# Split parts instead of activations through DRAM, and another order at the turn of the passes, in a hybrid decoder layer

## The chip, the cores and the metric

The kernel runs on one core of one Trainium2 chip. The metric is the device time in microseconds of one execution of the whole layer. Times below come from three runs, and from one further execution that the hardware profiler recorded.

## The reference

One decoder layer over 256 tokens of width 2048 in float32: a combined projection, two groups of eight attention heads (differential attention, and block attention that with 256 tokens is causal attention over one block), an output projection, LayerNorm, a gated FFN of width 5632 with a causal convolution of three taps, and a second LayerNorm. The change touches the FFN's down projection and what stands around it:

```python
def conv_ffn(h, w_up, conv_w, conv_b, w_down):
    u = h @ w_up
    g, val = u[..., :FFN_DIM], u[..., FFN_DIM:]
    ...
    gc = conv_b + sum(conv_w[j] * gp[:, j:j + S] for j in range(CONV_W))
    return (jax.nn.silu(gc) * val) @ w_down
...
f = conv_ffn(h, w_up[l], conv_w[l], conv_b[l], w_down[l])
h = layer_norm(DEEPNORM_ALPHA * h + f, ln2_g[l], ln2_b[l])
```

## The kernel before

**Precision.** A float32 operand is split in two fp32r parts: `hi`, a rounded copy (ScalarE), and `lo`, the operand less `hi` (VectorE). A product of two operands is three matmuls: hi by hi, hi by lo, lo by hi.

**Stream.** The weights come as a list of steps, `stream`, of 1 MB each: v, q/k, o, the up projection's g and u, and the down projection's d. Each step's weights are loaded by SyncE (`load`, lines L128 and L129 for a d step) into one of four `raw` tiles, which rotate, and split by `split` (L179 on ScalarE, L181 on VectorE) into one of six hi and six lo tiles.

**Down projection.** The inner dimension of 5632 makes 44 tiles of 128, taken as 22 pairs p (`PT`). The output of 256 x 2048 is more than the eight PSUM banks hold beside the shared products, so its columns are done in two passes n of 1024. A pass has the four blocks `CB[t][c]` (two row halves t, two column blocks c) in banks 0 to 3.

- *First pass (n = 0).* Pairs 0 to 19 are multiplied between the matmuls of the up projection (`up_step`, four steps a pair, q and s in the code; `down_products`), each by seven block products in place of eight (Winograd's form; the sums of activations in `side["s"]`, their parts in `side["sh"]` and `side["sl"]`). Banks 4 to 7 (`MB`) take the products that several blocks share. Pairs 20 and 21 follow as plain steps at `first_d` and `first_d` + 1.
- *Turn.* `z_add` adds the first pass's banks into the residual `z` (L1231), and `shared_out` adds the shared products (L1237, L1241, L1244). The second pass writes the same banks.
- *Second pass (n = 1).* The 22 pairs again, in order j = 0 to 21. Steps j = 2, 5, 8, 11, 14 are by seven products (`mm_seven`, 21 matmuls, blocks of weights prepared by `blocks_raw`, `blocks_lo`, `blocks_sum`, `blocks_hi` in `slot`), the others plain (`mm_d`, 24 matmuls). The last four pairs (`PAIRED_END`) are run column block by column block, so that the second LayerNorm can start.

**Activations.** `act_out` leaves a pair's activations in a ring of three. For the second pass `act_spill` (L506) writes them to DRAM (`spilled`, 256 KB a pair), and `act_back` (L513) reads them into `back` five steps ahead, on SyncE's queue in front of the weight load. `split_act` (L564 on ScalarE, L565 on VectorE) splits the two halves of a pair again, and for a seven-product step `act_sums` and `act_sums_split` (L583 to L586, L603, L604) form and split the sums again. The raw blocks' `lo` of a seven-product step is made by ScalarE's negated copy (L624) and an accumulating transfer from POOL's queue (L625).

**Order.** Each engine runs its instructions in the order in which the program issues them; waits are put in by the framework from the tiles' uses. `begin(i)` and `middle(i)` hold the preparation of step i + 2 (and the first half of i + 3); `at(i, ...)` hangs work on a step, run by `pending` after that step's splits. At step j = 9, `load_gb` (L467) loads the second LayerNorm's gain and bias, 1 MB each, on SyncE's queue. All matmuls of the projections are recorded at line L277.

The turn's work is hung on its steps by

```python
for part in range(2):
    at(first_d + part, shared_out, 0, part)
```

Of the kernel before, what the change touches and what calls it, by code (L numbers as in the profile page):

```python
# [11 lines left out]
F32 = mybir.dt.float32  # L12
# [40 lines left out]
ENDS = {(1, 1): ("cos_d", "sin_d"), (2, 0): ("mask", "lam4"), (2, 1): ("cos_m", "sin_m")}  # L53
# [6 lines left out]
def hymba_layer(ctx: ExitStack, tc: tile.TileContext, a: dict):  # L60
# [38 lines left out]
    for j, p in enumerate((*range(PT - LATE, PT), *range(PT - LATE))):  # L99
        stream.append(("d", p, 1, j))  # L100
# [133 lines left out]
    cst = {}  # L234

    def load_table(n):
        t = keep.tile([P, S], F32, name=n)
        SP.dma_start(t, a[n])
        cst[n] = t

    def load_consts():
        for n in ("cos_d", "sin_d", "mask"):
            load_table(n)
        lam4 = keep.tile([P, 4, SUB], F32, name="lam4")
# [244 lines left out]
    def act_ring():  # L489

        if "ring" not in kept:
            t = kept["ring"] = keep.tile([P, 4096], F32, name="ring", tag="mb")
            kept["raw"], kept["gb"] = t[:, 1536:3584], t[:, 3584:]
            kept["spilled"] = dram.tile([PT - LATE, P, 2, S], F32, name="spilled")
        return kept["ring"][:, 0:1536].rearrange("p (n k t) -> p n k t", k=2, t=S)
# [4 lines left out]
    def act_of(i, k):  # L500

        _, p, n, _ = stream[i]
        return kept["back"][:, p % 7, k] if n == 1 and p < PT - LATE else act_pair(p)[:, k]

    def act_spill(p):
        SP.dma_start(kept["spilled"][p], act_pair(p))  # L506

    def act_back(i):
        if i >= NS or stream[i][2] == 0 or stream[i][1] >= PT - LATE:
            return  # L510
        if "back" not in kept:
            kept["back"] = keep.tile([P, 8, 2, S], F32, name="back", tag="big")
        SP.dma_start(kept["back"][:, stream[i][1] % 7], kept["spilled"][stream[i][1]])  # L513
# [22 lines left out]
    aparts = {}  # L536
# [5 lines left out]
    def act_tiles(i, k):  # L542

        late = i - (NS - PAIRED_END)
        if (late, k) in ENDS:
            return [keep.tile([P, S], F32R, name="eh", tag=g) for g in ENDS[late, k]]
        if k == 0 and late < 3:
            return [work.tile([P, STAND_AT + S], F32R, name=n, tag=g, bufs=3)[:, STAND_AT:]
                    for n, g in (("ah", "e0"), ("al", "e1"))]
        if late < 1:  # L550
            return work.tile([P, S], F32R, name="bh", tag="pt"), work.tile([P, S], F32R, name="bl", tag="on")
        if k == 1 and i > first_d:
            both = work.tile([P, 2, S], F32R, name="chl", tag="sh", bufs=1)
        else:
            both = work.tile([P, 2, S], F32R, name="dhl", tag="m1")
        return both[:, 0], both[:, 1]

    def split_act(i, k):

        if i >= NS or stream[i][0] != "d" or (i, k) in aparts:  # L560
            return
        src = act_of(i, k)
        hi, lo = act_tiles(i, k)
        ACT.activation(hi, src, AF.Copy)  # L564
        DVE.tensor_tensor(lo, src, hi.bitcast(F32), ALU.subtract)  # L565
        aparts[i, k] = (hi, lo)
# [3 lines left out]
    sums = {}  # L570
    gap = []

    def act_sums(i):
        kind, p, _, _ = stream[i]
        if kind == "v":
            x = [xraw[:, k * S:(k + 1) * S] for k in (2 * p + 1, 2 * p)]
            f = work.tile([P, 2, 2, P], F32, name="vf", tag="sh", bufs=1)
            f = [f[:, 0], f[:, 1]]
        else:
            x = [act_of(i, k) for k in range(2)]  # L580
            f = [keep.tile([P, 2, P], F32, name="sf", tag=g) for g in ("cos_m", "sin_m")]
# [3 lines left out]
        DVE.tensor_tensor(f[1][:, 0], f[0][:, 1], a11, ALU.add)  # L585
        DVE.tensor_tensor(f[1][:, 1], a12, f[1][:, 0], ALU.subtract)  # L586
        sums[i] = f

    def act_sums_split(i):
        f = sums[i]  # L590
        out = []
        for j in range(2):
            if stream[i][0] == "d":
                hi = keep.tile([P, 2, P], F32R, name="sh", tag=("cos_d", "mask")[j])
                lo = keep.tile([P, 2, P], F32R, name="sl", tag=("sin_d", "lam4")[j])
            else:
                o = (STAND_AT, 0)[j]
                if j == 1 and not gap:

                    gap.append(work.tile([P, 8], F32, name="gap", bufs=1))  # L600
                hi, lo = (work.tile([P, o + S], F32R, name=n, tag=g, bufs=b)[:, o:].rearrange("p (k t) -> p k t", t=P)
                          for n, g, b in ((("vh", "e0", 3), ("vl", "e1", 3)), (("wh", "pt", 2), ("wl", "on", 2)))[j])
            ACT.activation(hi, f[j], AF.Copy)  # L603
            DVE.tensor_tensor(lo, f[j], hi.bitcast(F32), ALU.subtract)  # L604
            out += [(hi[:, k], lo[:, k]) for k in range(2)]

        sums[i] = out
# [3 lines left out]
    def blocks_raw(i):  # L611
# [3 lines left out]
        if kind == "d":  # L615
            slot = keep.tile([P, 2, 7, 512], F32R, name="slot", tag="t2")
            hi, lo = slot[:, 0], slot[:, 1]
# [6 lines left out]
        ACT.activation(lo[:, 0:3], t[:, 0:3], AF.Copy, scale=-1.0)  # L624
        POOL.dma_start(lo[:, 0:3], t[:, 0:3], accum_op=ALU.add)  # L625
# [10 lines left out]

    def blocks_sum(i, j):
# [5 lines left out]
        if j == 1:  # L643
            loaded.pop(i)
# [75 lines left out]
    def down_tiles():  # L720
# [3 lines left out]
        side["sh"] = [keep.tile([P, 2, P], F32R, name="sh", tag=g) for g in ("cos_d", "mask")]  # L724
        side["sl"] = [keep.tile([P, 2, P], F32R, name="sl", tag=g) for g in ("sin_d", "lam4")]
        side["x"] = [work.tile([P, S], F32R, name="xp", tag="pt") for _ in range(2)]
        side["a"] = work.tile([P, STAND_AT + S], F32R, name="ap", tag="e0", bufs=3)[:, STAND_AT:]
# [20 lines left out]
    def down_products(p):  # L748
        t, r, a1, (xh_, xl_) = side["t"], side["r"], side["a"], side["x"]
        sh, sl = side["sh"], side["sl"]  # L750
        (s3, s1), (s2, s4) = ([(sh[j][:, k], sl[j][:, k]) for k in range(2)] for j in range(2))
        a11, a12, a22 = (a1[:, 0:P], a1[:, P:]), (xh_[:, 0:P], xl_[:, 0:P]), (xh_[:, P:], xl_[:, P:])
# [33 lines left out]
    def begin(i):  # L786
# [3 lines left out]
        split_act(j - 1, 1)  # L790
        split_act(j, 0)
# [3 lines left out]
        elif j - 1 < NS and seven(j - 1):  # L795
# [324 lines left out]
    def up_step(i):  # L1120
# [18 lines left out]
        if s == 0 and now:  # L1139
            if "r" not in side:  # L1140
                side["r"] = keep.tile([P, 2, 3, 512], F32R, name="rslot", tag="big")
# [55 lines left out]
        if i >= first_d - 2:  # L1197
            split_act(i + 1, 1)
            split_act(i + 2, 0)
# [8 lines left out]
        if s == 0 and q >= 1 and q - 1 < PT - LATE:  # L1208
            act_spill(q - 1)
# [17 lines left out]
    act_out(FT - 1, up_sum(first_d - 1))  # L1227

# [4 lines left out]
    def shared_out(n, part):  # L1233

        u = kept["gb"] if n == 0 else kept["back"][:, 7].rearrange("p k t -> p (k t)")
# [37 lines left out]
    for part in range(2):  # L1273
        at(first_d + part, shared_out, 0, part)
    for i in range(first_d, NS - PAIRED_END):
# [4 lines left out]
        if i == last[0] - 1:  # L1280
            split_act(last[1], 1)
            for j, g in ((last[2], "t2"), (last[3], "mb")):
                end = keep.tile([P, 4, 1024], F32R, name="end", tag=g)
                for k in range(2):
                    split_act(j, k)
# [5 lines left out]
        else:  # L1291
# [10 lines left out]
            if n == 0 and p == PT - 1:  # L1302
# [101 lines left out]
    for c in range(2):  # L1404
        s = slice(c * 512, (c + 1) * 512)
        ACT.activation(z[:, 1, s], ends[c], AF.Copy, scale=rstd)
        store(1, c * 512, (c + 1) * 512)
# [72 lines left out]
```

## Time and profile before

| | |
|---|---|
| median of 3 runs | 1130.36 us (1129.09 to 1130.74) |
| the profiled execution | 1128.65 us, its span 1126.9 us |
| mean granted TensorE clock | 0.995 |
| TensorE busy | 1110.4 us (99%), 5929 matmuls |
| VectorE, ScalarE, POOL busy | 865.0, 702.9, 48.5 us |
| moved by DMA | 254.14 MB, 226 GB/s over the span |

The span is the time from the first to the last instruction of the core; the execution's own time has some 1.8 us around it. A busy TensorE is not TensorE at its peak, as matmuls overlap, so the count of matmuls in a stretch says more than its busy time. In a row of waits, the engine and line that waited stand first, then what ended the wait, then the total, the number of waits and the longest. In a row of stretches stand the stretch and its length, then for TensorE's matmuls, its weight loads, VectorE, ScalarE and POOL the busy time with the number of instructions, then the granted clock, the share of time in which the 16 DMA engines were busy, and GB/s. In a row of a group the figures behind the bar are busy time and the mean of one in ns, then the idle time before them with what ended it. Queue q1 is that of the transfers that SyncE starts, q0 that of POOL's.

### The profile page before, as it was taken

How to read it: one execution, taken by the hardware profiler on the slowest of the kernel's cores; microseconds unless marked ns; L12 is line 12 of the kernel's file. 1: busy time of each engine (PE TensorE's matmuls, PEld its weight loads, DVE VectorE, ACT ScalarE, POOL GpSimd, SP SyncE). 2: the span in 40 equal slices, each digit the busy share in tenths (PEclk: the TensorE clock that was granted, in tenths of full speed). 3: DMA queues.
4: the chain of work that ended last, by engine and by line, in shares of the span. 5: the costliest groups of instructions: out<-in, count | busy, mean ns of one | idle time of the engine just before them, and what ended most of it. 6: DMA issues, size and time to landing. Idle time of an engine off the chain costs nothing.

```text
span 1126.9 us, 15881 instructions
## 1 busy us (share of the span) xinstructions
PE 1110.4 (99%) x5929; PEld 955.0 (85%) x5929; DVE 865.0 (77%) x1469; ACT 702.9 (62%) x1136; POOL 48.5 (4%) x61
## 2 busy tenths in 40 slices
PE   9999999999999999999999999999999999989987
PEld 7888888888888898888888888888888888868875
DVE  6776778877745779888888877777777777698776
ACT  6666776644533577666666666666666666657662
POOL 0000110000000000000000000000000000000003
PEclk9999999999999999999999999999999999999999
DMA  9889766444455448777766877777777777578962
GB/s 341 273 276 326 225 188 205 150 157 179 172 182 201 156 162 273 246 250 239 234 234 234 278 236 239 229 232 241 238 231 228 233 224 223 170 232 240 311 260 76
DMA packets 58860, 254.14 MB, mean 226 GB/s; under 512 B 5968, under 2 KB 7456, under 8 KB 40992
## 3 DMA queue, kind: packets, MB, share of 16 engines
q1 hardware_dynamic: 53600, 226.92, 56.0%
q0 software_dynamic: 5184, 26.22, 12.4%
q8 instruction: 46, 0.75, 0.3%
q14 instruction: 30, 0.25, 0.1%
HBM read 219.80 MB, written 7.08 MB: 201 GB/s over the span
## 4 chain that ended last, share of the span: by engine, by line
PE 94%; DVE 2%; DMA 1%; ACT 1%; issue 1%; SPq 0%; DVEq 0%
PE bank L277 93%; DMA back<-spilled 1%; PE bank L404 0%; DVE lo L181 0%; DVE z L1231 0%; ACT hi L179 0%; PE bank L975 0%; PE bank L451 0%; ACT hf L978 0%; ACT slot L624 0%; ACT slot L630 0%; ACT ah L564 0%; DVE h L990 0%; DVE slot L635 0%; ACT bh L564 0%
## 5 line engine op out<-in xcount | busy, mean ns | idle before, releaser
L277 PE MATMUL bank<-h,hi 128*128 128x512 f32 x1376 | 480.9, 390 | 0.0
L277 PE MATMUL bank<-h,lo 128*128 128x256 f32 x1376 | 387.9, 282 | 0.0
L277 PEld LDWEIGHTS bank<-h,hi 128*128 128x128 f32 x1376 | 258.2, 188 | 54.5
L277 PEld LDWEIGHTS bank<-h,lo 128*128 128x128 f32 x1376 | 260.0, 189 | 3.7
L181 DVE TENSOR_TENSOR lo<-raw,hi 128x1024 fp32r<-128x1024 f32 x147 | 177.9, 1222 | 83.9 <-ACT hi L179 83.2
L198 DVE TENSOR_TENSOR lo<-raw,hi 128x1024 fp32r<-128x1024 f32 x171 | 206.9, 1221 | 25.0 <-ACT hi L190 24.9
L179 ACT ACTIVATE hi<-raw 128x1024 fp32r<-128x1024 f32 x155 | 162.9, 1055 | 78.2 <-PE bank L277 54.0
L277 PE MATMUL bank<-x,hi 128*128 128x512 f32 x512 | 183.4, 399 | 0.0
L190 ACT ACTIVATE hi<-raw 128x1024 fp32r<-128x1024 f32 x171 | 177.3, 1051 | 0.0
L277 PE MATMUL bank<-x,lo 128*128 128x256 f32 x512 | 144.3, 282 | 0.0
L1095 ACT ACTIVATE ub<-bank 128x512 f32<-128x512 f32 x86 | 51.4, 598 | 111.1 <-PE bank L277 108.1
L277 PEld LDWEIGHTS bank<-x,hi 128*128 128x128 f32 x512 | 96.2, 188 | 21.9 <-issue 2.3
L277 PEld LDWEIGHTS bank<-x,lo 128*128 128x128 f32 x512 | 96.8, 189 | 0.2
L1104 DVE TENSOR_TENSOR ub<-ub 128x256 f32<-128x256 f32 x86 | 36.5, 424 | 57.8 <-ACT ub L1095 57.8
L730 ACT ACTIVATE tslot<-tf 128x512 fp32r<-128x512 f32 x80 | 50.4, 629 | 40.9 <-DVE tf L1184 22.2
L733 DVE TENSOR_TENSOR tslot<-tf,tslot 128x512 fp32r<-128x512 f32 x80 | 55.3, 691 | 12.3 <-ACT tslot L730 10.3
L277 PE MATMUL bank<-hi,x 128*128 128x512 f32 x208 | 56.5, 394 | 0.0
L277 PEld LDWEIGHTS bank<-hi,x 128*128 128x128 f32 x208 | 39.4, 190 | 8.7 <-ACT hi L210 0.3
L277 PE MATMUL bank<-hi,mh 128*128 128x512 f32 x128 | 41.2, 394 | 0.0
L277 PE MATMUL bank<-lo,mh 128*128 128x512 f32 x128 | 40.8, 390 | 0.0
L277 PE MATMUL bank<-hi,ml 128*128 128x512 f32 x128 | 40.8, 389 | 0.0
L531 ACT ACTIVATE gc<-gc 128x256 f32<-128x256 f32 x44 | 18.4, 418 | 35.0 <-DVE gc L528 35.0
(281 smaller groups left out, 1589.5 us busy)
## 6 DMA issues: line engine op xcount, KB each, us to landing
raw<-in_w_u SPq DMA_DIRECT2D x88, 1024.0 KB, 4.8
raw<-in_w_d SPq DMA_DIRECT2D x68, 512.0 KB, 6.9
raw<-in_w_qk SPq DMA_DIRECT2D x32, 1024.0 KB, 4.8
raw<-in_w_o SPq DMA_DIRECT2D x16, 1024.0 KB, 4.9
raw<-in_w_v SPq DMA_DIRECT2D x28, 512.0 KB, 8.9
ring<-in_w_d SPq DMA_DIRECT2D x20, 512.0 KB, 7.8
rslot<-raw POOLq DMA_DIRECT2D x10, 768.0 KB, 6.9
rslot<-ring POOLq DMA_DIRECT2D x10, 768.0 KB, 6.4
```

The source lines that it names most:

```text
L179: ACT.activation(hi[:, s], t[:, x:y], AF.Copy)
L181: DVE.tensor_tensor(lo[:, s], t[:, x:y], hi[:, s].bitcast(F32), ALU.subtract)
L190: ACT.activation(hi, t[:, half * 1024:half * 1024 + 1024], AF.Copy)
L198: DVE.tensor_tensor(lo, t[:, half * 1024:half * 1024 + 1024], hi.bitcast(F32), ALU.subtract)
L277: PE.matmul(out, lhsT, rhs, start=start, stop=stop)
L531: ACT.activation(gates[f], gates[f], AF.Silu)
L730: ACT.activation(side["t"][:, 0, j], f, AF.Copy)
L733: DVE.tensor_tensor(side["t"][:, 1, j], f, side["t"][:, 0, j].bitcast(F32), ALU.subtract)
L1095: ACT.activation(t.rearrange("p j t -> p (j t)"), up_bank(i), AF.Copy)
L1104: DVE.tensor_tensor(u[:, 0], u[:, 0], u[:, 1], ALU.add)
```

## The change

The parts that the first pass has split are kept, instead of the activations. The parts of a pair's two halves now stand together in `side["x"]` (both halves whole), and the sums' parts in `side["sp"]`. `act_spill` writes `side["x"]` (512 KB a pair) to `dparts`, and for the five pairs that are by seven products in the second pass `side["sp"]` (512 KB) to `dsums`. `act_back` reads them on POOL's queue, three steps ahead, into tiles that TensorE reads directly; the second pass's `split_act`, `act_sums` and `act_sums_split` are gone. Pairs 20 and 21 (`LATE` = 2) are split once and their parts serve both passes. The seven-product steps move by one (j = 3, 6, 9, 12, 15). In a d step the raw blocks' `lo` is made by VectorE (`blocks_lo_raw`), not by the accumulating transfer. `shared_out` of the first pass hangs two steps later, and the statistics of the finished half of `z` four and six steps later. One of the last stores goes out from ScalarE's queue. Some small tables share one tile (`four`), whose place the sums' parts take later.

```diff
-SEVEN = {"v": ((), range(1, 8, 3)), "d": (range(PT - 2), range(2, 15, 3))}
-LATE = 3
+SEVEN = {"v": ((), range(1, 8, 3)), "d": (range(PT - 2), range(3, 16, 3))}
+LATE = 2
...
-    for j, p in enumerate((*range(PT - LATE, PT), *range(PT - LATE))):
+    for j, p in enumerate((*range(PT - LATE, PT), PT - LATE - 1, *range(PT - LATE - 1))):
...
+            kept["parts"], kept["sums"] = (dram.tile([PT - LATE, P, 4, S], F32R, name=n) for n in ("dparts", "dsums"))
...
     def act_spill(p):
-        SP.dma_start(kept["spilled"][p], act_pair(p))
+        SP.dma_start(kept["parts"][p].bitcast(F32), side["x"].bitcast(F32))
+        if p in sevens:
+            SP.dma_start(kept["sums"][p].bitcast(F32), side["sp"].bitcast(F32))
...
     def act_back(i):
...
-        SP.dma_start(kept["back"][:, stream[i][1] % 7], kept["spilled"][stream[i][1]])
+            kept["back"] = keep.tile([P, 4, 4, S], F32R, name="back", tag="big")
+        t = down_slot()[:, 14:].rearrange("p a (b t) -> p (a b) t", t=S) if i == NS - 1 else kept["back"][:, j % 4]
+        POOL.dma_start(t, kept["parts"][p])
+        for h in range(2):
+            aparts[i, h] = t[:, 2 * h], t[:, 2 * h + 1]
+        if seven(i):
...
+            t = kept["sback"][:, j % 2]
+            POOL.dma_start(t, kept["sums"][p])
...
     def act_sums(i):
...
+        if kind == "d":
+            return
...
     def blocks_raw(i):
...
-        ACT.activation(lo[:, 0:3], t[:, 0:3], AF.Copy, scale=-1.0)
-        POOL.dma_start(lo[:, 0:3], t[:, 0:3], accum_op=ALU.add)
+        if kind == "v":
+            ACT.activation(lo[:, 0:3], t[:, 0:3], AF.Copy, scale=-1.0)
+            POOL.dma_start(lo[:, 0:3], t[:, 0:3], accum_op=ALU.add)
...
+    def blocks_lo_raw(i):
+        if stream[i][0] == "d":
+            hi, lo, _ = blocks[i]
+            t = raws_of.pop(i).rearrange("p (b c) -> p b c", c=512)
+            DVE.tensor_tensor(lo[:, 0:3], t[:, 0:3], hi[:, 0:3].bitcast(F32), ALU.subtract)
...
     def begin(i):
...
-        split_act(j - 1, 1)
-        split_act(j, 0)
...
             blocks_lo(j - 1, 3)
+            blocks_lo_raw(j - 1)
...
-            act_back(i + 5)
+            act_back(i + 3)
         load(i + 6)
...
     def up_step(i):
...
         if s == 1 and now:
-            x, (xh_, xl_), a1 = act_pair(p), side["x"], side["a"]
-            ACT.activation(xh_, x[:, 1], AF.Copy)
-            DVE.tensor_tensor(xl_, x[:, 1], xh_.bitcast(F32), ALU.subtract)
-            ACT.activation(a1[:, 0:P], x[:, 0, 0:P], AF.Copy)
-            DVE.tensor_tensor(a1[:, P:], x[:, 0, 0:P], a1[:, 0:P].bitcast(F32), ALU.subtract)
+            x, y = act_pair(p), side["x"]
+            for h in (1, 0):
+                ACT.activation(y[:, 2 * h], x[:, h], AF.Copy)
+                DVE.tensor_tensor(y[:, 2 * h + 1], x[:, h], y[:, 2 * h].bitcast(F32), ALU.subtract)
...
-        if i >= first_d - 2:
-            split_act(i + 1, 1)
-            split_act(i + 2, 0)
+        if i == first_d - 2:
+            split_act(first_d, 0)
+        if i == first_d - 1:
+            split_act(first_d, 1)
+            split_act(first_d + 1, 0)
...
-        if s == 0 and q >= 1 and q - 1 < PT - LATE:
-            act_spill(q - 1)
+        if s == 1 and now:
+            act_spill(p)
...
     for part in range(2):
-        at(first_d + part, shared_out, 0, part)
+        at(first_d + LATE + part, shared_out, 0, part)
...
-                        at(i + 2 + t, z_stats, t, c, (512, 256)[t])
+                        at(i + 6 + 3 * t, z_stats, t, c, (512, 256)[t])
...
-        store(1, c * 512, (c + 1) * 512)
+        if c == 0:
+            store(1, 0, 512)
+        else:
+            ACT.dma_start(out[1][:, 512:1024], z[:, 1, 512:1024])
```

More of the change, by code (lines that the diff above doesn't have):

```diff
@@ L234, in hymba_layer @@
     cst = {}
+    FOUR = {"cos_d": 0, "sin_d": 1, "mask": 2}
     def load_table(n):
-        t = keep.tile([P, S], F32, name=n)
+        t = cst["four"][:, FOUR[n]] if n in FOUR else keep.tile([P, S], F32, name=n)
         SP.dma_start(t, a[n])
@@ L241, in load_consts @@
     def load_consts():
+        cst["four"] = keep.tile([P, 4, S], F32, name="four")
         for n in ("cos_d", "sin_d", "mask"):
             load_table(n)
-        lam4 = keep.tile([P, 4, SUB], F32, name="lam4")
+        lam4 = cst["four"][:, 3].rearrange("p (a b) -> p a b", b=SUB)
         vec = keep.tile([P, N_COLS], F32, name="vec")
@@ L510, in act_back, with down_slot @@
             return
+        _, p, _, j = stream[i]
         if "back" not in kept:
-            kept["back"] = keep.tile([P, 8, 2, S], F32, name="back", tag="big")
-        SP.dma_start(kept["back"][:, stream[i][1] % 7], kept["spilled"][stream[i][1]])
+            kept["back"] = keep.tile([P, 4, 4, S], F32R, name="back", tag="big")
[4 more added lines that the diff above has]
+        if seven(i):
+            if "sback" not in kept:
+                kept["sback"] = keep.tile([P, 2, 4, S], F32R, name="sback", tag="mb")
+            t = kept["sback"][:, j % 2]
+            POOL.dma_start(t, kept["sums"][p])
+            sums[i] = [(t[:, 2 * h, k * P:(k + 1) * P], t[:, 2 * h + 1, k * P:(k + 1) * P]) for h in range(2)
+                       for k in range(2)]
+    def down_slot():
+        if "slot" not in kept:
+            kept["slot"] = keep.tile([P, 16, 512], F32R, name="slot", tag="t2")
+        return kept["slot"]
     gates = {}
@@ L534, in act_out @@
         DVE.tensor_tensor(act_pair(f // 2)[:, f % 2], u, gates.pop(f), ALU.mult)
-    aparts = {}
+    aparts, sums = {}, {}
+    sevens = [p for kind, p, n, j in stream if (kind, n) == ("d", 1) and j in SEVEN["d"][1]]
     def seven(i):
@@ L540, in seven @@
         return kind in SEVEN and (j if kind == "d" else p) in SEVEN[kind][n] and (kind, n) != ("d", 0)
[L542 to L556, printed above, removed]
-    def split_act(i, k):
[L560 to L563, printed above, removed]
+    def split_act(i, k):
+        _, p, n, _ = stream[i]
+        hi, lo = (work.tile([P, S], F32R, name=n, tag="pt") if (p, k) == (PT - 1, 1) else
+                  work.tile([P, STAND_AT + S], F32R, name=n, tag=g, bufs=3)[:, STAND_AT:]
+                  for n, g in (("ah", "e0"), ("al", "e1")))
+        src = act_pair(p)[:, k]
         ACT.activation(hi, src, AF.Copy)
         DVE.tensor_tensor(lo, src, hi.bitcast(F32), ALU.subtract)
-        aparts[i, k] = (hi, lo)
-    sums = {}
+        for j, (kind, q, _, _) in enumerate(stream):
+            if kind == "d" and q == p:
+                aparts[j, k] = (hi, lo)
     gap = []
@@ L574, in act_sums @@
         kind, p, _, _ = stream[i]
[L575 to L581, printed above, removed]
+        if kind == "d":
+            return
+        x = [xraw[:, k * S:(k + 1) * S] for k in (2 * p + 1, 2 * p)]
+        f = work.tile([P, 2, 2, P], F32, name="vf", tag="sh", bufs=1)
+        f = [f[:, 0], f[:, 1]]
         a11, a21, a12, a22 = (x[k][:, t * P:(t + 1) * P] for k in range(2) for t in range(2))
@@ L592, in act_sums_split @@
         for j in range(2):
[L593 to L602, printed above, removed]
+            o = (STAND_AT, 0)[j]
+            if j == 1 and not gap:
+                gap.append(work.tile([P, 8], F32, name="gap", bufs=1))
+            hi, lo = (work.tile([P, o + S], F32R, name=n, tag=g, bufs=b)[:, o:].rearrange("p (k t) -> p k t", t=P)
+                      for n, g, b in ((("vh", "e0", 3), ("vl", "e1", 3)), (("wh", "pt", 2), ("wl", "on", 2)))[j])
             ACT.activation(hi, f[j], AF.Copy)
@@ L615, in blocks_raw @@
         if kind == "d":
-            slot = keep.tile([P, 2, 7, 512], F32R, name="slot", tag="t2")
-            hi, lo = slot[:, 0], slot[:, 1]
+            slot = down_slot()
+            hi, lo = slot[:, 0:7], slot[:, 7:14]
         else:
@@ L643, in blocks_sum @@
         if j == 1:
-            loaded.pop(i)
+            raws_of[i] = loaded.pop(i)
     def blocks_hi(i, j):
@@ L723, in down_tiles @@
         side["s"] = [keep.tile([P, 2, P], F32, name="sf", tag=g) for g in ("cos_m", "sin_m")]
[L724 to L727, printed above, removed]
+        side["sp"] = keep.tile([P, 4, S], F32R, name="sp", tag="four")
+        side["sh"], side["sl"] = ([side["sp"][:, 2 * j + i].rearrange("p (k t) -> p k t", t=P) for j in range(2)]
+                                  for i in range(2))
     def t_hi(j, f):
@@ L1140, in up_step @@
             if "r" not in side:
-                side["r"] = keep.tile([P, 2, 3, 512], F32R, name="rslot", tag="big")
+                t = keep.tile([P, 4096], F32R, name="rslot", tag="big")
+                side["r"] = t[:, 0:3072].rearrange("p (a b c) -> p a b c", b=3, c=512)
+                side["x"] = t[:, 3072:].rearrange("p (a t) -> p a t", t=S)
             w = raw_of(p)
@@ L1227, in hymba_layer @@
     act_out(FT - 1, up_sum(first_d - 1))
+    split_act(first_d + 1, 1)
     def z_add(n, t, c, src):
@@ L1233, in shared_out @@
     def shared_out(n, part):
-        u = kept["gb"] if n == 0 else kept["back"][:, 7].rearrange("p k t -> p (k t)")
+        if part == 0:
+            kept["u"] = work.tile([P, 512], F32, name="u", tag="sh", bufs=1)
+        u = kept["u"]
         if part == 0:
@@ L1280, in hymba_layer @@
         if i == last[0] - 1:
-            split_act(last[1], 1)
-            for j, g in ((last[2], "t2"), (last[3], "mb")):
-                end = keep.tile([P, 4, 1024], F32R, name="end", tag=g)
+            act_back(last[3])
+            ends = (down_slot()[:, 0:8].rearrange("p (a b) c -> p a (b c)", b=2),
+                    keep.tile([P, 4, 1024], F32R, name="end", tag="mb"))
+            for j, end in zip(last[2:], ends):
                 for k in range(2):
-                    split_act(j, k)
                     split(j, k, end)
```

13 lines of the change are left out of this document (6 added, 7 removed).

## The prediction

> **What bounds the kernel now.** I read the page's busy times and queues first, then who waited for whom, then the stretches of the second pass, then the order of time around each stall.
>
> ```profile
> span 1126.9 us, 15881 instructions
> PE 1110.4 (99%) x5929; PEld 955.0 (85%) x5929; DVE 865.0 (77%) x1469; ACT 702.9 (62%) x1136; POOL 48.5 (4%) x61
> q1 hardware_dynamic: 53600, 226.92, 56.0%
> q0 software_dynamic: 5184, 26.22, 12.4%
> ...
> PE bank L277 <- DVE z L1231: 3.8, 1, 3.8
> PE bank L277 <- ACT slot L648: 3.0, 1, 3.0
> PE bank L277 <- DVE slot L635: 0.6, 1, 0.6
> ...
> 406.00:900.00 494.00, 494.00 (x2735) 431.97 (x2734) 395.83 (x623) 332.79 (x495) 15.52 (x18) 1.00 0.74 242
> 978.00:1005.00 27.00, 23.09 (x94) 18.48 (x94) 24.79 (x45) 17.16 (x27) 0.86 (x1) 0.94 0.53 160
> 1005.00:1020.00 15.00, 15.00 (x68) 12.43 (x67) 14.39 (x29) 10.53 (x17) 0.86 (x1) 1.00 0.94 305
> 1020.00:1035.00 15.00, 15.00 (x67) 12.40 (x67) 12.80 (x25) 11.00 (x18) 0.86 (x1) 1.00 0.83 268
> 1035.00:1050.00 15.00, 15.00 (x68) 12.43 (x67) 12.67 (x25) 11.43 (x18) 0.86 (x1) 1.00 0.86 261
> 1050.00:1065.00 15.00, 15.00 (x68) 12.43 (x67) 12.66 (x24) 10.17 (x16) 0.86 (x1) 1.00 1.01 316
> 1065.00:1080.00 15.00, 11.42 (x43) 8.72 (x42) 8.25 (x14) 7.23 (x11) 0.00 (x0) 0.89 1.03 358
> 978.00:1095.00 117.00, 109.50 (x466) 89.30 (x466) 94.20 (x165) 75.89 (x121) 4.30 (x5) 0.97 0.80 260
> ```
>
> TensorE bounds the kernel; there is nothing to win where it runs without a gap (494.00 of 494.00 us in most of the up projection). In the second pass it is let down twice. Undisturbed it starts 68 + 67 + 68 + 68 = 271 matmuls in four stretches of 15 us, 0.221 us each. The 27 us at the turn hold 94 where 122 would fit: 28 x 0.221 = 6.2 us lost. The stretch from 1065 holds 43 where 67.75 would: 24.75 x 0.221 = 5.5 us. That is more than the waits (3.8, and 3.0 + 0.6), because the granted clock falls too: (1 - 0.94) x 27 = 1.6 us and (1 - 0.89) x 15 = 1.7 us. Together 11.7 us: all that the change can win on TensorE.
>
> **The stall at the turn.** In order of time, VectorE and TensorE:
>
> ```profile
> 988.04 0.61 PE L277 MATMUL bank<-hi,bl 128*128 128x512 f32 x2
> 988.96 0.68 DVE L1231 TENSOR_TENSOR z<-z,ring 128x512 f32<-128x512 f32 x1
> 989.68 0.69 DVE L1244 TENSOR_TENSOR ring<-bank,ring 128x512 f32<-128x512 f32 x1
> 990.40 1.29 DVE L1231 TENSOR_TENSOR z<-z,ring 128x512 f32<-128x512 f32 x2
> 991.61 1.87 DVE L1231 TENSOR_TENSOR z<-z,bank 128x512 f32<-128x512 f32 x3
> 992.44 0.47 PE L277 MATMUL bank<-hi,ah 128*128 128x512 f32 x1 [3.79 <-DVE z L1231]
> ...
> L635 DVE TENSOR_TENSOR slot<-tf,slot 128x512 fp32r<-128x512 f32 x20 | 13.7, 684 | 0.0
> L181 DVE TENSOR_TENSOR lo<-raw,hi 128x1024 fp32r<-128x1024 f32 x30 | 36.6, 1221 | 11.1 <-ACT hi L179 11.1
> ```
>
> The next pass writes banks 0 and 1 first. The two additions that empty them are the first of those at 991.61, behind the shared sums (the rows on ring). The change puts the eight shared operations (some 0.69 us each, 5.5 us) two steps later and drops four of the halves' splits of activations that stood here. The first two bank additions can then run as soon as their products end, before TensorE has finished the other half of that step (12 x 0.221 = 2.7 us); the other two are 1.3 us of VectorE after 988.5 and are wanted 2.7 us after it. I take the whole 6.2 us; bounds 0 and 6.2. Late next is the first seven-product step, now one step later (j = 3). From 988.5 VectorE has two bank additions, eight shared ones and eight block operations (18 x 0.69), four splits (4 x 1.22) and the new subtraction (1.8, below): 19.1 us by their rows, some 18 in a row, as two of 0.69 take 1.29. TensorE comes to the product that needs the last of them after 3 x 24 + 12 matmuls, 18.6 us. So the cover is about half a us; if it is gone, TensorE waits for the rest there.
>
> **The stall at 1070.**
>
> ```profile
> 1055.74 15.11 DMA back<-spilled
> 1070.87 0.42 ACT ah L564
> ...
> SPq L128 <- DMA slot<-raw: 45.6, 5, 12.2
> SPq L513 <- DMA gb<-in_ln_g: 2.7, 1, 2.7
> ...
> raw<-in_w_d SPq DMA_DIRECT2D x68, 512.0 KB, 6.9
> back<-spilled SPq DMA_DIRECT2D x19, 256.0 KB, 8.6
> slot<-raw POOLq DMA_DIRECT2D x5, 768.0 KB, 10.4
> ...
> L564 ACT ACTIVATE ah<-back 128x256 fp32r<-128x256 f32 x17 | 6.8, 402 | 7.4 <-DMA back<-spilled 7.4
> L565 DVE TENSOR_TENSOR al<-back,ah 128x256 fp32r<-128x256 f32 x17 | 7.1, 419 | 5.9 <-ACT ah L564 5.9
> L604 DVE TENSOR_TENSOR sl<-sf,sh 128x256 fp32r<-128x256 f32 x10 | 3.8, 418 | 0.0
> L585 DVE TENSOR_TENSOR sf<-sf,back 128x128 f32<-128x128 f32 x4 | 1.2, 292 | 0.1
> ```
>
> A 256 KB read of the activations takes 15.11 us, because SyncE's queue is held by the accumulating transfer of each seven-product step (45.6 us in five waits) and then starts the gain and bias (2 x 1024 KB) and two steps' weights at once. ScalarE and VectorE, in order, stand behind the split of those activations. The change removes each link: no accumulation in this pass, no split behind the read, and the read on POOL's queue, three steps ahead. Two plain steps of 24 matmuls and one of 21 are 69 x 0.221 = 15.2 us of lead, against 10.4 us that POOL's 768 KB took to land. I take the 5.5 us as won; bounds 0 and 5.5.
>
> **What it adds.** *DMA time* is the disputed cost. By the queue rows a MB costs 0.560 x 1126.9 / 226.92 = 2.78 us of all 16 engines on q1 and 0.124 x 1126.9 / 26.22 = 5.33 us on q0 (POOL's, all of it accumulating). Taken out: 5 x 0.786 MB on q0 (21.0 us) and 19 x 0.262 MB on q1 (13.8 us). Put in: 20 parts and 5 sums of 0.524 MB, 13.1 MB on POOL: 36.4 us at q1's price, 69.9 us at q0's. Net +1.6 or +35 us on the 0.80 x 117 = 93.6 us of this stretch, 105 us long once the stalls are gone. I take +1.6: an accumulation reads two streams, a plain read one, so q1's row is the nearer. The new reads then hide as the old ones did; at q0's price there is no cover. In the DMA-full stretches (1.01, 1.03) the 2.1 MB of gain and bias are still 5.8 us that weights queue behind, and the weights of the step after a seven-product step are now loaded only once VectorE has read that step's raw tile a last time. Bounds for a wait left there 0 and 5.5 us; I take 1.5, nearer to 0, as the activations no longer queue there.
>
> *VectorE and ScalarE.* Out: 44 splits of halves (0.42 and 0.40 us), five steps' sums with their splits, five negations; in: five subtractions of 128x1536 (L181's 1.22 us x 1.5 = 1.8 us). VectorE sheds 18.5 us (44 x 0.42), 10 (five times four of 0.29 and two of 0.42) less 9, ScalarE more. Off the path, 0. *The up projection:* the first factor is split whole, +0.1 us on each engine for 20 pairs; VectorE is at 395.83 of 494 us: 0. Spilling parts writes 0.26 MB more per pair, and 0.52 MB more for five of them, at a DMA share of 0.74: 0. SyncE waits for that split before it spills, and the weight load behind it waited already for a later VectorE split: 0. *TensorE:* as many steps by seven products (five), the same matmuls; loaded stationaries in place of split ones, price 0. *Later z statistics* (six operations on VectorE): 0. *One last store from ScalarE's queue:* the last of four in a row is started one start earlier.
>
> ```profile
> 1120.40 1.41 DVE L1331 SCALAR_TENSOR_TENSOR z<-z,rstd,gb 128x512 f32<-128x512 f32 x2
> 1120.52 1.26 ACT L1406 ACTIVATE z<-bank,rstd 128x512 f32<-128x512 f32 x2 [0.64 <-PE bank L277]
> 989.49 0.47 SPq L129 DMA_DIRECT2D raw<-in_w_d  x1
> ```
>
> A start takes some 0.47 us: -0.4, bounds 0 and -0.5.
>
> **Sum.** The profiled execution took 1128.65 us (span 1126.9); the median of the runs is 1130.36, 1.7 more. 1128.65 - 6.2 - 5.5 + 1.5 - 0.4 = 1118.0; against the median, **1119.7**.
>
> **Two rules of the Trainium skill.** The clock rows above cost 1.6 and 1.7 us, half of 3.3 us each. The Trainium skill, "TensorE: Matmul & The Clock Gate", Part 1, says that an idle window of about 3.4 us halves the clock and a busy one restores it; the trace agrees with the halving. By that rule a leftover wait of 1.5 us would cost itself alone, as in the sum; were the clock to fall with it, the sum would be 1.7 higher, 1121.4. Against the change speaks "DMA: Bandwidth & Descriptors", Issuing engines are not separate DMA queues: the Trainium skill says that transfers from different engines share the same 16 DMA engines, and another queue saves only issue time. The trace agrees in so far as the shares around 1065 reach 1.03 with both queues at work; what it would do here is the second rival.
>
> **Rivals.** *(1) POOL's reads cost what its accumulations cost.* Place: every step of the second pass. For: q0's row is the only price of that queue, and the new reads make fp32r out of DRAM. Against: one stream less. Three steps then need 3 x 1.05 MB x 2.78 = 8.8 us of weights and four pieces at 2.8 us, 20 us of DMA against 15.2 us of TensorE.
>
> ```profile
> 1080.00:1095.00 15.00, 15.00 (x68) 12.42 (x67) 8.64 (x12) 8.36 (x15) 0.00 (x0) 1.00 0.62 235
> L181 DVE TENSOR_TENSOR end<-raw,end x4: 1214/1214/1215, 1094.0 to 1098.4; 128x1024 fp32r<-128x1024 f32 x4
> ```
>
> 93.6 + 35 = 129 us from 978 end at 1107 at the earliest, where the transfers before ended near 1089 (0.62 x 15 = 9.3 us after 1080); of these 18 us some 7 are the lead that the last weights had (they are split from 1094.0 to 1098.4). Slower: about 1130.4 + 11 = 1141. It decides from about 2.1 us a piece: 25 x 0.65 us more use up the 105 - 93.6 - 1.6 = 10 us of free DMA time and that lead.
>
> *(2) The second stall forms again behind the gain and bias,* on weights rather than on activations. For: shares of 1.01 and 1.03 with the 2.1 MB still there. Against: no accumulations, no split in the chain. Only the turn is won: 1130.4 - 6.2 - 0.4 = 1123.8.
>
> *(3) The turn does not open:* the additions are placed first, but VectorE comes late to the first seven-product step. Then 5.5 + 0.4 - 1.5 are won: 1126.
>
> **Chances.** The forecast 0.60, with a range of its own of 1117 to 1122; rival 2 0.15, rival 3 0.07, rival 1 0.13 with prices in between that cancel the gain, 0.05. 0.2% (2.3 us) is about what a measurement of this kernel can tell from no change. Faster 0.82, same 0.05, slower 0.13. The range, 1116 to 1128, goes from the whole 11.7 us won with nothing left (1130.36 - 12.1 = 1118, less 2 us for the spread of runs) to a gain just above that limit; rival 1 is left out.
>
> **What would show it.** No wait of TensorE on z at L1231's place, and 122 starts in the 27 us after 978; POOL's parts landing in under 10 us with q0's price per MB near 2.8 us; no wait over 2 us on the last seven-product step (j = 15); clock rows at 1.00 up to the last layer norm. A price per MB on q0 near 5 us, or TensorE waiting for parts at every third step, would make the prediction wrong.

## The result, and the profile after

The changed kernel takes 1121.3 us (median of four runs, 1119.24 to 1121.72) against 1129.94 us of the kernel before on the same chip: the ratio is 0.992, with a 95% interval from 0.9903 to 0.9937. The forecast was 1119.7. The profiled execution took 1121.72 us, the highest of the four, where that of before (1128.65) lay under all four of its runs; read from the two profiles the gain is 6.9 us, from the medians 8.6.

The page of the changed kernel, its groups of DMA issues, and TensorE's waits between 900 and 1100:

```profile
span 1119.9 us, 15776 instructions
PE 1108.7 (99%) x5929; PEld 953.2 (85%) x5929; DVE 853.4 (76%) x1400; ACT 681.6 (61%) x1077; POOL 57.5 (5%) x81
q0 software_dynamic: 8064, 35.39, 14.1%
...
back<-dparts POOLq DMA_DIRECT2D x19, 512.0 KB, 7.2
...
PE bank L277 <- ACT slot L658: 0.7, 1, 0.7
PE bank L277 <- DVE slot L643: 0.7, 1, 0.7
PE bank L277 <- DVE slot L637: 0.5, 1, 0.5
```

The wait of 3.8 us on `z` is gone; in its place stands nothing. The waits of 3.0 and 0.6 us in the last seven-product step have become three of 0.7, 0.5 and 0.7. What that is worth is seen from the starts in each stretch:

```profile
978.00:1005.00 27.00, 27.00 (x121) 22.35 (x120) 21.59 (x31) 13.87 (x17) 2.69 (x5) 1.00 0.69 239
1005.00:1020.00 15.00, 15.00 (x68) 12.43 (x67) 11.60 (x14) 7.83 (x11) 2.11 (x4) 1.00 0.85 302
1065.00:1080.00 15.00, 12.95 (x47) 9.40 (x47) 10.47 (x10) 6.54 (x7) 1.05 (x2) 0.89 0.85 300
978.00:1095.00 117.00, 114.95 (x497) 93.90 (x496) 87.41 (x107) 55.30 (x65) 13.25 (x25) 0.99 0.84 298
```

The turn holds 121 starts where 94 stood: it is won but for one start of the 122. The stretch from 1065 holds 47 of the 67.75 that fit: 20.75 x 0.221 = 4.6 us are still lost, where 5.5 were. Of these, 1.9 are the three waits and 1.7 the lower clock (below); about 1 us stands in no row of waits. The first seven-product step (j = 3, between 1005 and 1020) loses nothing.

The chain of waits shows what holds j = 15 now. Its columns are start, length, and what the chain went through; rows between are left out, and the row under the dots is from TensorE's own order of time:

```profile
1006.29 1.68 DVE slot L643
1008.45 7.17 DMA raw<-in_w_d
1021.09 1.68 DVE slot L643
1023.24 8.20 DMA raw<-in_w_d
1036.85 1.68 DVE slot L643
1039.00 8.54 DMA raw<-in_w_d
1053.00 1.68 DVE slot L643
1055.16 11.64 DMA raw<-in_w_d
1066.88 1.07 ACT hi L177
1068.01 1.11 issue
1072.27 1.68 DVE slot L643
1073.99 36.54 PE bank L277 x176
...
1007.47 2.20 PE L277 MATMUL bank<-slot,back 128*128 128x512 f32 x9
```

It is a loop that closes over DMA: VectorE's new subtraction (L643) reads the raw tile last, SyncE starts the weights that want that tile, they land, ScalarE and VectorE split them, and the next subtraction stands behind those splits. From one subtraction to the next, j = 3 to j = 15, the rounds take 14.8, 15.8, 16.2 and 19.3 us, against 15.2 us of TensorE's work in three steps: all but the first are longer, so the lead shrinks round by round and is used up at j = 15. No row of the parts is in it. The lead is small from the start: at j = 3 the subtraction ends at 1007.97, and the first matmul that needs its result, the fifth of the nine in the last row, starts near 1008.4.

### The profile page after: what moved, and what is told of

It is laid out like the page before. It is cut to its first block, busy times and chain, and to the rows that moved or that the text cites. A ratio compares the mean times of both kernels' runs of the same rounds, so it can differ in the third digit from the quotient of the medians.

```text
span 1119.9 us, 15776 instructions
## 1 busy us (share of the span) xinstructions
PE 1108.7 (99%) x5929; PEld 953.2 (85%) x5929; DVE 853.4 (76%) x1400; ACT 681.6 (61%) x1077; POOL 57.5 (5%) x81
## 4 chain that ended last, share of the span: by engine, by line
PE 90%; DMA 4%; DVE 4%; issue 1%; ACT 1%; SPq 0%; DVEq 0%; ACTq 0%
PE bank L277 90%; DMA raw<-in_w_d 3%; DVE slot L643 1%; DVE lo L179 1%; DVE slot L637 1%; DMA raw<-in_w_v 0%; ACT hi L177 0%; PE bank L404 0%; DVE z L1244 0%; PE bank L984 0%; PE bank L451 0%; SPq L126 0%; DVE tf L652 0%; ACT hf L987 0%; DVE h L999 0%
## 5 line engine op out<-in xcount | busy, mean ns | idle before, releaser
L179 DVE TENSOR_TENSOR lo<-raw,hi 128x1024 fp32r<-128x1024 f32 x147 | 177.1, 1221 | 98.9 <-ACT hi L177 98.3
L277 PE MATMUL bank<-hi,back 128*128 128x512 f32 (+1 forms) x216 | 58.9, 381 | 0.0
L277 PE MATMUL bank<-tslot,sp 128*128 128x512 f32 x180 | 47.8, 392 | 0.0
L277 PEld LDWEIGHTS bank<-hi,back 128*128 128x128 f32 x216 | 40.2, 188 | 7.9
```

The source lines that it names most:

```text
L179: DVE.tensor_tensor(lo[:, s], t[:, x:y], hi[:, s].bitcast(F32), ALU.subtract)
L277: PE.matmul(out, lhsT, rhs, start=start, stop=stop)
```

## The experiments

Losses below are counted as above: 122 starts fit into the 27 us from 978, 67.75 into 15 us, and each missing one is 0.221 us. The medians of the experiments belong to three series of runs, in which the kernel before took 1129.12, 1130.29 and 1129.38 us; each ratio is taken within its series.

| kernel | median us | ratio to before (95%) | lost from 978 to 1020, us | lost from 1065 to 1080, us |
|---|---|---|---|---|
| before | 1129.94 | 1 | 6.1 | 5.5 |
| changed | 1121.3 | 0.992 (0.9903 to 0.9937) | 0.2 | 4.6 |
| before, order | 1130.47 | 1.0008 (0.9999 to 1.0018) | 6.8 | 6.1 |
| before, order and j = 3 | 1125.07 | 0.995 (0.9938 to 0.9962) | 3.5 | 4.4 |
| before, gain early | 1124.07 | 0.9948 (0.9933 to 0.9963) | 7.0 | 0 |
| before, order and gain early | 1123.93 | 0.9949 (0.9934 to 0.9964) | 6.8 | 0 |
| before, order, j = 3, gain early | 1120.14 | 0.9914 (0.99 to 0.9927) | 3.0 | 0 |
| changed, order undone | 1122.47 | 0.9934 (0.9919 to 0.9948) | 5.0 | 0.4 |
| changed, order undone, gain early | 1121.46 | 0.9932 (0.9919 to 0.9944) | 5.0 | 0.2 |
| changed, gain early | 1116.91 | 0.9891 (0.9876 to 0.9907) | 0.4 | 0 |
| changed, raw tile free early | 1117.26 | 0.9893 (0.9879 to 0.9906) | 0.8 | 0.2 |
| changed, both early | 1117.29 | 0.9888 (0.9873 to 0.9903) | 0.6 | 0 |

**The order alone, in the kernel before.**

```diff
-        at(first_d + part, shared_out, 0, part)
+        at(first_d + 2 + part, shared_out, 0, part)
```

> The kernel before with one edit: the shared sums of the first pass hang two steps later, as after the change; activations, accumulations and the rest as before. Theory A (the turn is lost by the order of VectorE's work alone): the 6.2 us at the turn come back, 1129.9 - 6.2 = 1123.7 us, the wait at 1070 stays. Rival B (VectorE is short of time at the turn, and only the splits that the parts save make room): the wait moves to the first seven-product step, at or over 1128 us.

Nothing was won. TensorE's largest wait, and where it stands in the order of time:

```profile
PE bank L277 <- DVE ring L1244: 4.6, 1, 4.6
...
1004.74 0.69 DVE L1244 TENSOR_TENSOR ring<-bank,ring 128x512 f32<-128x512 f32 x1
1005.48 1.20 PE L277 MATMUL bank<-slot,sh 128*128 128x512 f32 x2 [4.58 <-DVE ring L1244]
```

The turn itself is open (no wait on L1231), but the first seven-product step, here j = 2, writes the banks of the shared products again, and the last shared operations (L1244) now come after it wants them. The wait moved by two steps, to where rival B expected it; the next run tests rival B's reason.

**The same, and the seven-product steps one step later.**

```diff
-SEVEN = {"v": ((), range(1, 8, 3)), "d": (range(PT - 2), range(2, 15, 3))}
+SEVEN = {"v": ((), range(1, 8, 3)), "d": (range(PT - 2), range(3, 16, 3))}
```

> The kernel before with two of the change's edits: the shared sums of the turn two steps later, and the seven-product steps one step later (j = 3, 6, 9, 12, 15 in place of 2 to 14). Activations still go through DRAM and are split again, the accumulating transfers stay. Where the order alone was changed, TensorE's wait only moved: from 3.8 us at the turn to 4.6 us in the first seven-product step (j = 2), on the bank that line L1244 empties. Theory A: the turn needs the order and one plain step more between it and the first seven-product step (24 matmuls, 5.3 us, more than the 4.6 us), and nothing of the parts: the 6.2 us of the turn are won, about 1123.5, 0.9945 of before, and no wait over 0.7 us stands from 978 to 1010. Rival B: it is the VectorE work that the parts take away (18.5 us in the second pass) that makes the room; without it a wait of 3 to 5 us stays at the turn or at j = 3, and the time is 1127 to 1130.

Both theories were half right. From 978 to 1005 there are 120 starts, so one plain step more does open the turn without any parts. But then j = 3 itself is late:

```profile
978.00:1005.00 27.00, 27.00 (x120) 22.37 (x120) 24.47 (x44) 16.83 (x26) 0.86 (x1) 1.00 0.68 208
1005.00:1020.00 15.00, 12.92 (x54) 9.79 (x53) 14.52 (x28) 11.50 (x19) 0.86 (x1) 1.00 0.70 233
...
1000.95 1.28 DVE L1253 BATCH_NORM_STATS2 st<-z 128x6 f32<-128x512 f32 x2
```

54 starts of 67.75 are 3.0 us lost, with VectorE at 14.52 of 15 us, where the changed kernel has it at 11.60 and loses nothing. From 988 on, ahead of the last block of j = 3, VectorE has here the activations' splits and sums, some 3.8 us by the starts of its instructions, which the change takes away, and also two operations of the statistics of `z` (the last row, 1.2 us), which the change hangs later. Which of the two makes the room was not separated.

**The order undone, in the changed kernel** (`shared_out` at `first_d + part`).

> The changed kernel with the shared sums of the first pass hung where they were before. Theory A: the wait on z at the turn is back, less the splits that VectorE no longer has there (four of 0.42 us), so 4.5 to 6.2 us worse: 1125.8 to 1127.5 us. Rival B: the parts alone make room, at most 1123 us.

Only 1.2 us are lost, which is rival B's time, but the turn waits again, as theory A has it:

```profile
PE bank L277 <- DVE z L1244: 2.8, 1, 2.8
...
978.00:1005.00 27.00, 24.07 (x99) 19.31 (x98) 22.75 (x33) 14.05 (x18) 2.69 (x5) 0.94 0.71 238
1065.00:1080.00 15.00, 15.00 (x66) 12.09 (x65) 10.00 (x10) 6.56 (x7) 1.58 (x3) 1.00 0.91 319
```

23 starts (5.1 us) are lost at the turn and almost none at j = 15. A TensorE that comes five microseconds late to the crowded stretch finds its weights there. So it seems that what the order wins at the turn is for the most part given back at j = 15; a run below tests it.

**Gain and bias early.** In the kernel before:

```diff
-        if n == 1 and j == 9:
+        if n == 0 and p == PT - 1:
             load_gb(2, keep.tile([P, 2, D], F32, name="gb2", tag="ma"))
```

> The kernel before with one edit: gain and bias of the second LayerNorm (2.1 MB) are loaded at the turn, behind the last first-pass pair's loads, and not at the second pass's step 9. Theory A (the wait at 1070 is the 2.1 MB on a nearly full DMA, whatever stands behind them): the 5.5 us come back, 1124.4 us, the wait at the turn stays. Rival C (the accumulations that hold SyncE's queue are the cause): no change or another wait in its place, 1129 to 1131 us.

> The kernel before with both edits: shared sums two steps later, gain and bias at the turn; activations still go through DRAM and are split again, accumulations stay. Theory A: both losses gone, 1129.9 - 11.7 = 1118.2 us, under the changed kernel's 1121.3. Rivals B and C: over 1121.3, as the parts or the missing accumulations are needed.

> The same, and the load of gain and bias moved from the step j = 9 to the turn. Theory A (the two stalls are both matters of order): 6.2 + 5.5 us won with nothing sent through DRAM as parts, about 1118, 0.990 of before, and so 2 to 3 us under the changed kernel. Rival B (the turn needs the parts): only the gain and bias count, as with that edit alone, 1123.5 to 1124.

With this one edit the kernel before is 5.0 us faster (1129.12 - 1124.07) and has no second stall, as theory A has it, although the accumulations hold SyncE's queue for longer than before (55.7 us in place of 45.6). With the order besides, nothing more is won, far from theory A's 1118.2 (the wait of 4.6 us on L1244 is there again). With the order and j = 3 the time is 1120.14. SyncE's wait in the first of these kernels, and the stretch of j = 3 in the last:

```profile
SPq L128 <- DMA slot<-raw: 55.7, 5, 12.4
...
1005.00:1020.00 15.00, 12.94 (x55) 9.85 (x54) 14.51 (x28) 11.51 (x19) 0.86 (x1) 1.00 0.75 243
```

So three edits of one line each, with nothing of the parts, bring as much as the whole change. The theory's 1118 was missed by the 2.8 us that j = 3 loses here (55 starts).

In the changed kernel gain and bias go from j = 9 to j = 0:

```diff
-        if n == 1 and j == 9:
+        if n == 1 and j == 0:
```

> The changed kernel with the load of gain and bias at step j = 0 in place of j = 9, nothing else. The stall that is left at the last seven-product step (j = 15) costs 4.6 us: three waits of 1.9 us in all, half the clock for 3.4 us and what lies around them. Theory A: it comes from the weights of one step that land 11.6 us after their start, because 2 MB of gain and bias stand in the same DMA engines; moved away, that landing falls to 7 to 9 us and the 4.6 us are won: about 1116.7, 0.9885 of before, no wait of TensorE over 0.3 us after 1050. Rival B: it is the loop through the raw tile itself (the weights' load may start only when VectorE has read the tile a last time), which would keep the waits: 1120 to 1121.5.

Theory A holds: TensorE has no wait at all between 978 and 1100, and all stretches are full.

```profile
978.00:1005.00 27.00, 27.00 (x120) 22.35 (x120) 21.62 (x30) 14.05 (x18) 2.69 (x5) 1.00 0.89 318
1065.00:1080.00 15.00, 15.00 (x68) 12.43 (x67) 8.73 (x8) 6.53 (x8) 2.11 (x4) 1.00 0.97 340
```

At 1116.91 it is faster than both kernels, 3.2 us under the kernel before with the three edits: the 2.8 us at j = 3 and the store below.

> The changed kernel with the shared sums of the turn at their old steps, as in the run that undid the order alone (1122.5), and besides with gain and bias loaded at step j = 0. With the order undone alone, TensorE lost 23 starts (5.1 us) at the turn and none at j = 15, where the changed kernel loses 4.6 us. Theory A (what the order wins at the turn is given back at j = 15, as TensorE then comes five microseconds earlier into the stretch in which the DMA engines are full): with gain and bias out of that stretch nothing is given back, and the order is worth its full 5 us: 1121.5 to 1122.5 here against 1116.9 with gain and bias early alone. Rival B (the order is worth about 1.2 us whatever stands behind it): 1118 to 1118.5.

The median is 1121.46, as theory A says. With gain and bias out of the way the order is worth 1121.46 - 1116.91 = 4.6 us, and the intervals of the two ratios lie apart; with them in the way the medians differ by 1.2 us, and the intervals overlap.

**The raw tile free early**, gain and bias at j = 9: the subtraction moves ahead of the next step's second split, in `begin`.

```diff
             blocks_sum(j - 1, 1)
+            blocks_lo_raw(j - 1)
             split(j, 1)
             blocks_hi(j - 1, 1)
             blocks_lo(j - 1, 3)
-            blocks_lo_raw(j - 1)
```

> The changed kernel, gain and bias at j = 9 as they were, with the raw blocks' lo of a seven-product step subtracted ahead of the next step's second split on VectorE: the raw tile is free about 1.9 us sooner, and so the weights of the step after next start sooner. Theory A (the stall at j = 15 is 1.9 us of waiting at the end of a loop of reads, splits and loads, and any 1.9 us of room in it takes it away): 1116.7 to 1118. Rival B (in the DMA-full stretch a sooner start lands no sooner, the engines being taken by gain and bias): 1120.5 to 1121.5, the landing of the last loop's weights 13 to 14 us in place of 11.6.

The chain of waits around the last round:

```profile
1048.80 0.38 SPq L126
1049.23 13.89 DMA raw<-in_w_d
...
1066.85 0.83 DVE slot L643
```

The landing became longer, 13.89 us, as rival B said; the time is that of theory A. The rounds add up: these weights start at 1048.80 where they started at 1054.73, 5.9 us sooner, and land only 2.3 us more slowly. So the stall had two causes that were each needed, a loop without spare time and 2 MB in its way, and to remove either is enough.

> The changed kernel with gain and bias at step j = 0 and, besides, the seven-product step's raw blocks' lo subtracted ahead of the next step's second split on VectorE, which frees the raw tile about 1.9 us sooner. Theory A (gain and bias alone made the stall): as with gain and bias alone, 1116.7, within 0.3 us of it. Rival B (the loop through the raw tile is short of room by itself): 0.5 to 4 us faster than with gain and bias alone, 1116.5 to 1117.5 where that one stays at 1120 to 1121.5.

1117.29, within 0.4 us of either edit alone: nothing is left to win there.

**The disputed DMA time.** Two kernels put a cost back. In one, the accumulating transfer makes the raw blocks' `lo` of the d steps again, as before the change, and VectorE's subtraction is left out:

```diff
-        if kind == "v":
-            ACT.activation(lo[:, 0:3], t[:, 0:3], AF.Copy, scale=-1.0)
-            POOL.dma_start(lo[:, 0:3], t[:, 0:3], accum_op=ALU.add)
+        ACT.activation(lo[:, 0:3], t[:, 0:3], AF.Copy, scale=-1.0)
+        POOL.dma_start(lo[:, 0:3], t[:, 0:3], accum_op=ALU.add)
```

> The changed kernel with one part of the change undone: the raw blocks' lo of the five seven-product steps made by ScalarE's negated copy and the accumulating transfer from POOL's queue again, not by VectorE's subtraction. By the row of before, 5 x 0.786 MB at 5.33 us a MB are 21 us of all DMA engines more in the stretch from 978, that is 0.84 x 117 + 21 = 119 us of transfers in about 111 us of work. Theory A (the parts' reads fit only because the accumulations went): 1126 to 1135, waits of TensorE at j = 9 to 15, and waits of SyncE's queue on the accumulation of over 10 us a step. Rival B (the transfers have room enough, and VectorE's five subtractions, 9 us, were no gain): within 1 us of the changed kernel, 1120.5 to 1122.

1130.45 us (ratio 1.0011, 0.9999 to 1.0023): the whole gain is gone, as theory A has it. The profiled execution, at 1127.25, is the fastest of this kernel's ten. Its rows of POOL's queue, of SyncE's wait and of the stretch:

```profile
q0 software_dynamic: 8784, 39.33, 15.7%
...
SPq L126 <- DMA slot<-raw: 59.6, 5, 12.7
...
978.00:1095.00 117.00, 111.48 (x474) 89.89 (x473) 74.35 (x94) 59.92 (x67) 17.80 (x30) 0.97 0.99 332
```

The DMA engines are busy for 0.99 of the 117 us. By the queue rows 3.94 MB of accumulation cost 0.157 x 1125.5 - 0.141 x 1119.9 = 18.8 us, 4.8 us a MB. Two things are mixed in this kernel: the full engines, and the raw tile, which SyncE finds free only when the accumulation has landed (59.6 us in five waits). In the kernel before with gain and bias early, the second alone made no stall (55.7 us of such waits); how the loss divides here was not separated.

In the other, every part is read a second time into a tile that nobody reads:

```diff
         POOL.dma_start(t, kept["parts"][p])
+        if "again" not in kept:
+            kept["again"] = keep.tile([P, 4, S], F32R, name="again", tag="four")
+        POOL.dma_start(kept["again"], kept["parts"][p])
```

> The changed kernel with every part of the second pass read twice from DRAM, the second time into a tile that nobody uses: 20 x 0.524 MB more on POOL's queue. It is the price of the first rival (about 5.5 us a MB) put upon the same reads. By POOL's queue rows the plain reads cost 2.8 to 3.0 us a MB, so 29 to 31 us more of all DMA engines, 128 us of transfers from 978 on in about 111 us of work. Theory A (there were about 10 us of free DMA time and some 7 us of lead, as in the working of that rival): 1133 to 1141, with waits of TensorE on weights and parts from j = 6 on. Rival B (reads from a second queue find room beside the weights): under 1126.

1136.71 us (ratio 1.0061, 1.0045 to 1.0076), in theory A's range. But theory A expected TensorE to wait on weights as well, and there is no such wait:

```profile
q0 software_dynamic: 10944, 45.88, 16.6%
...
PE bank L277 <- DMA sback<-dsums: 8.6, 2, 8.0
PE bank L277 <- DMA back<-dparts: 3.7, 2, 2.3
PE bank L277 <- DMA slot<-dparts: 2.7, 1, 2.7
...
POOL again L517 <- DMA again<-dparts: 89.7, 18, 7.4
...
978.00:1095.00 117.00, 108.41 (x466) 88.63 (x465) 81.14 (x98) 52.87 (x61) 21.25 (x40) 0.96 1.00 359
```

10.49 MB of plain reads cost 0.166 x 1135.7 - 0.141 x 1119.9 = 30.6 us, 2.9 us a MB, and leave the DMA engines no idle time in the stretch. One thing is mixed in, and it may be most of the loss: the second reads share one tile, so POOL's queue waits for each of them to land (89.7 us in all), and the parts and sums behind it start later. TensorE's waits of 8.6 + 3.7 + 2.7 = 15.0 us are all on these reads, and the kernel is 15.4 us slower than the changed one. How much of it the full engines would cost alone was not separated.

## Why the prediction was right, and where not

The time came 1.6 us from the forecast, inside its own range of 1117 to 1122. The sum behind it was not right in every term, and two things hid that: the second stall kept most of its cost, and the two profiled executions stood differently to their medians (1.3 us under, 0.4 us over). In the profiled executions' own time the forecast was 1118.0 and the second rival 1128.65 - 6.2 - 0.4 = 1122.05; measured were 1121.72. By mechanism, rival 2 is what happened; that the number still fell nearer to the forecast, and inside its range, is in part luck.

- *The turn, 6.2 us:* 27 of the 28 missing starts are won, 6.0 us, near the upper bound. But the step that says how is too short. It gives the new order and four splits fewer as the reason; the order alone wins nothing. It takes the order, the seven-product steps one later, and less VectorE work before j = 3.
- *The cover of half a us at j = 3:* it held, and it was as thin as worked out (1007.97 against 1008.4). With the order and the step alone 2.8 to 3.0 us are lost there. To name that step as "late next" was the most useful line of this part, and it should have been weighed as a condition of the 6.2 us, not beside them.
- *The second stall, 5.5 us less 1.5:* this is the term that failed. Left was 4.6, not 1.5; 0.9 us were won of the forecast 4.0. The step was "The change removes each link". It removed the read of activations, their split and the accumulation, and put in a link of its own: the raw tile is held until VectorE's subtraction. The prediction has this link (weights "loaded only once VectorE has read that step's raw tile a last time") and the 2.1 MB of gain and bias, but prices each as a remainder, and does not go round the loop that they form. Of each of the four rounds 7.6 us are not landing (16.15 - 8.54 in the third); with a landing of 6.9 us, the median of before, that is 14.5, just under the 15.2 of three steps of TensorE, and with any landing over 7.6 it is more. The reading of the stall before was off in the same place: it put SyncE's waits on the accumulations first, and with gain and bias early the stall is gone while those waits are longer. And the sign named for it, no wait over 2 us at j = 15, was met with 4.6 us still lost; the count of starts shows the stall, the longest wait does not.
- *Given back:* the prediction adds the two stalls as if they were independent. They are not. Whatever is won at the turn brings TensorE earlier to the stretch where DMA has no reserve (4.6 us against 1.2 for the same edit).
- *The clock:* the prediction let the leftover wait cost itself alone, and gave 1121.4 if the clock fell with it. It fell:

```profile
1070.35:1073.76 3.41, 1.71 (x6) 0.67 (x4) 3.41 (x4) 2.53 (x3) 0.00 (x0) 1.00 0.75 278
1073.76:1077.17 3.41, 3.18 (x8) 2.50 (x9) 3.41 (x4) 2.00 (x2) 0.38 (x1) 0.50 0.55 126
```

  A stretch of 3.41 us in which TensorE was busy for 1.71 is followed by one of the same length at 0.50: 1.7 us, nearly as much as the three waits (1.9 us) themselves. The Trainium skill, "TensorE: Matmul & The Clock Gate", Part 1, speaks of an idle window of about 3.4 us that halves the clock; the length agrees, but here a window that was half busy was enough.
- *DMA time, +1.6 us net at q1's price:* right: the stretch from 978 has a share of 0.84 after 0.80, with 497 matmuls in it after 466; that is 98.3 us of transfers after 93.6, where the first rival had 129. The first rival's price is refuted for plain reads (2.9 us a MB, not 5.3). Its threshold of 2.1 us a piece stays open: with twice the reads, 2.9 x 2 x 0.524 = 3.0 us a piece, the kernel is slower than before, but the waits of POOL's queue are in that. A second queue brought no second supply of transfers, as the Trainium skill has it in "DMA: Bandwidth & Descriptors", Issuing engines are not separate DMA queues: in the two kernels with a cost put back, the shares of the 16 engines stand at 0.99 and 1.00 of the stretch with both queues at work. Parts land in 7.2 us (median), under the 10 us that were asked for. Moreover the net is small only because the accumulations went: with them back, the transfers fill the stretch and the gain is zero.
- *VectorE, ScalarE, up projection: 0.* VectorE's relief, or the later statistics that were also priced 0, is what keeps the 2.8 us at j = 3; the sentence "Off the path, 0" is wrong there. The relief was right in durations (19.5 us less the 2 of the up projection; VectorE's groups add up to some 17 us less), but as busy time it was over-sized: the page shows 865.0 - 853.4 = 11.6, as neighbouring instructions overlap. The up projection runs without a gap as before.
- *The last store, -0.4 us:* right. From ScalarE's last pass over `z` (L1421, L1406 before) to the end of the span it is 1119.9 - 1113.93 = 6.0 us after and 1126.9 - 1120.52 = 6.4 before.

```profile
1113.93 1.26 ACT L1421 ACTIVATE z<-bank,rstd 128x512 f32<-128x512 f32 x2 [0.65 <-PE bank L277]
1114.65 1.30 SPq L1349 DMA_DIRECT2D out<-z  x3
1115.23 0.38 ACTq L1425 DMA_DIRECT2D out<-z  x1
```

Of the 6.9 us between the profiles, 6.0 are the turn, 0.9 the second stall and 0.4 the tail; 0.6 go the other way at a wait on the first weights, in a part that the change does not touch, and 0.2 are left over.

## What to carry to other kernels

Follow a stall round its loop: a tile's last reader, the transfer that waits for it, its landing and the splits behind it; if the round is longer than the work it must keep up with, a link taken out buys little while another is put in. Two stalls in a row are not two terms of a sum: time won at the first is taken from the lead at the second, so clear the later one first, and then the earlier edit shows its worth. Before work is taken off the engines, look for the one large transfer that can stand in an idle stretch: two loads moved ten steps ahead made the kernel before 5 us faster, more than half of what the whole rewrite did.

## What had not been expected of the hardware

The clock fell after a window that was half busy, and did not fall after two that were 0.7 busy: in the kernel before with the three edits, three waits of 2.1 us in all lie at j = 3, more than the 1.9 us above, and the clock stays at 1.00.

```profile
1004.95:1008.37 3.42, 2.41 (x10) 1.36 (x8) 3.34 (x6) 1.82 (x5) 0.00 (x0) 1.00 0.25 62
1008.37:1011.78 3.41, 2.36 (x9) 1.74 (x10) 3.41 (x7) 2.94 (x5) 0.00 (x0) 1.00 0.66 168
1110.77:1114.18 3.41, 0.83 (x3) 0.29 (x2) 2.33 (x4) 1.53 (x3) 0.00 (x0) 1.00 0.81 321
1114.18:1117.59 3.41, 0.00 (x0) 0.00 (x0) 0.00 (x0) 0.00 (x0) 0.00 (x0) 0.50 0.60 217
...
PE bank L277 <- ACT slot L648: 1.2, 1, 1.2
PE bank L277 <- DVE slot L635: 0.9, 2, 0.6
```

These stretches are laid in steps of 3.41 us back from where that run's clock last changed (1114.18): the waits fall into two windows, each busy for 2.4 us, while the clock changed behind one that was busy for 0.83. That the clock goes by such fixed windows, and so by how the waits happen to fall into them, would fit both runs; it was not tested.
